# The first stage of a one-core decoder step: another order of loads, sessions and products

## The chip, the cores and the metric

The kernel runs on one core of one Trainium2 chip. The metric is the device time of one execution in microseconds; less is better. Three runs of the kernel before took 1009.87, 1010.07 and 1011.35 us, a median of 1010.07 us.

## The reference, cut to what matters

One layer of a hybrid decoder over 512 prompt tokens and 8 sample tokens (520 columns, D = 1024), all in float32:

```python
cs  = silu(c)                                   # 9 conditioning rows: 1 prompt, 8 samples
mod = cs @ w_mod + b_mod                        # (9, 6*1024): shift1, scale1, gate1, shift2, scale2, gate2
h   = rmsnorm(x, norm1_g) * (1 + scale1) + shift1
u   = h @ w_in                                  # 8 blocks of 1024 columns: q f i og x y ga gb
f   = lb + (1 - lb) * sigmoid(fa);  k = (1 - lb) * sigmoid(-fa);  q = silu(qa)
S_t = diag(f_t) S_{t-1} + k_t (x) v_t;  o_t = S_t^T q_t     # 8 heads of 128, v = ia
o_a = rmsnorm(o) * silu(oga);  o_b = RG-LRU(conv(xb)) * gelu(yb)
x   = x + gate1 * (sig(ga) * (o_a @ w_branch_a) + sig(gb) * (o_b @ w_branch_b)) @ w_out
x   = x + gate2 * (relu(h2 @ w_ff1)^2 @ w_ff2);  y = rmsnorm(x)   # h2 from x as h, with shift2, scale2
```

The part that concerns the change is everything up to `h` and the first column tiles of `u`.

## The kernel before, in words

Activations lie transposed: 8 feature columns (tiles k of 128 features on the partitions) by 520 tokens. A gemm makes one tile of 128 output features: 8 products, one per k, each of six matmuls. The operands are split into a high and a low part (`hi` is the rounded value, `lo` the rest), and a product is high by high, high by low and low by high, each over two halves of 260 tokens (`products`, L112). Weights come as tiles of 512 KB on the SP queue (`_load_w`), are cast to `whi` on ScalarE (L84) and subtracted to `wlo` on VectorE (L87), two tiles ahead of their gemm (`take_w`). The PSUM pool `pmm` has two buffers, so the third gemm needs the first one's result read.

The first stage (`begin`, L1579) makes `h` and the first two column tiles, which are f and q of head 0. SP loads c, x, then blocks of w_mod of 256 columns (1 MB each: scale1, part 1, and shift1, part 0, for two feature columns), with the two 512 KB tiles of w_in among them. ScalarE takes the squares of x, TensorE transposes x in pairs of feature columns (L462), VectorE takes the inverse root (L445 to L198); the root is transposed to all partitions (L470), copied (L474), and the columns are scaled by it (L477). Four conditioning sessions follow, one per pair of feature columns: 32 matmul records over two blocks of w_mod (L382), a copy to SBUF on ScalarE (L385), four transposes (L397) and reductions on VectorE (L402 to L409) give scale and shift. Then `affine_split` (L480) makes the pair's high columns on ScalarE (L490, tail L494), its full columns (L495) and low columns (L496) on VectorE. Between a session and its transposes stands the first of the last pair's four products, behind the transposes the other three. Only some orders are fixed, by dependencies without a wait (`behind`); the rest is set by the planner of the tile framework, which orders each engine's list by its own timeline.

Tiles of the stage lie in the pool `start`, which is closed at its end; the pool `hg` of the heads is opened over the same memory, and its first tiles wait for everything that read `start`. Then each head runs its gemms (f, q, output gate, v), sigmoids of f first (L157 by `head_f`), and leaves the rest of the recurrence to VectorE, ScalarE and small matmuls: v's copy (L549), its transposes and its broadcast over DRAM (`head_sample_v`), the decay levels (`level`, the last one ending in L618), the keys' transposes (L694). Parts that depend on them (`keys`, `states`, ...) are queued by `later(n, part)`, to be issued behind the n-th gemm from there. Two gemms of the RG-LRU branch stand between two heads.

Of the kernel before, what the change touches and what calls it, by code (L numbers as in the profile page):

```python
# [15 lines left out]
D = 1024  # L16
L = 512
# [13 lines left out]
NWM = 8  # L31
# [20 lines left out]
class Kernel:  # L52
    def __init__(self, ctx, tc, ins, outs):
        self.ctx, self.tc, self.nc = ctx, tc, tc.nc
        self.i, self.o = ins, outs
        self.group, self.sigmoids, self.mod_open = None, [], None
        self.ppt_free = True
        self.rg_pending = self.turn = self.last_hi = self.split_last = None
        self.late, self.ngemm = [], 0
# [18 lines left out]
    def _split_w(self, st, place, after=None, after_lo=None):  # L78
# [5 lines left out]
        ins = self.nc.scalar.copy(hi, st)  # L84
        if after:
            self.behind(ins, after)
        ins = self.nc.vector.tensor_tensor(lo, st, hi.bitcast(F32), OP.subtract)  # L87
        if after_lo:
            self.behind(ins, after_lo)
        return hi, lo  # L90

    def split_place(self):

        self.nsplit += 1
        self.places.append(self.nsplit % 4 if self.sw else 2 * (self.nsplit % 3))
        return self.places[-1]

    def take_w(self, key):
        n = self.wcur
        assert self.wspecs[n] == key, (n, self.wspecs[n], key)  # L100
        while self.wnext_split < min(n + AHEAD + 1, len(self.wspecs)):
# [7 lines left out]
        self.wcur += 1  # L109
        return self.wsplit.pop(n)  # L110
# [76 lines left out]
    def rsqrt_small(self, x, n, p=128, w=16):  # L187
# [4 lines left out]
        nc.vector.tensor_scalar(t.bitcast(I32), x.bitcast(I32), 1, None, OP.arith_shift_right)  # L192
        nc.vector.tensor_scalar(y.bitcast(I32), t.bitcast(I32), -1.0, float(0x5F3759DF), OP.mult, OP.add)
        nc.vector.tensor_scalar(h, x, -0.5, None, OP.mult)
        for _ in range(3):
            nc.vector.tensor_tensor(t, y, y, OP.mult)
            nc.vector.tensor_tensor(t, t, h, OP.mult)
            nc.vector.scalar_tensor_tensor(y, t, 1.5, y, OP.add, OP.mult)  # L198
# [39 lines left out]
    def transpose_in(self, out, rows, n):  # L238

        nc = self.nc  # L240
        ps = self.pps.tile([128, 512], F32, name="ps")
        nc.tensor.transpose(ps[:, :n], rows[:n, :], self.ident[:n, :n])
        nc.vector.tensor_copy(out, ps[:, :n])

# [9 lines left out]
    def bounds(self, r):  # L254

        nc = self.nc
        pl = self.hc.tile([128, 16], F32, name="pl")
        self.transpose_in(pl, r, 16)
        hl, lam = pl[:, 0:8], pl[:, 8:16]

        sb = self.hc
        t = sb.tile([128, 10, 8], F32, name="ptmp")
        mx, e, p, lb, na, ex, s, s2, acc, d = (t[:, j] for j in range(10))
        nc.vector.tensor_copy(mx, hl)
        nc.vector.tensor_tensor(e, hl, mx, OP.subtract)
        nc.vector.tensor_scalar(d, lam, -1.0, None, OP.mult)
        nc.vector.tensor_tensor(na, lam, d, OP.min)
        nc.scalar.activation(e, e, AF.Exp)
        self.exps = nc.scalar.activation(ex, na, AF.Exp)
        nc.vector.reciprocal(p, e)  # L270
        nc.vector.tensor_tensor(p, p, e, OP.mult)
        nc.vector.tensor_tensor(lb, p, p, OP.subtract)
        self.lbf, self.lb1, self.c8, self.c8n = (sb.tile([128, 8], F32, name=n) for n in ("lbf", "lb1", "c8", "c8n"))
        nc.vector.tensor_scalar(self.lbf, lb, 1e-30, None, OP.max)
        nc.vector.tensor_scalar(self.lb1, lb, -1.0, 1.0, OP.mult, OP.add)
        self.decay = ex, s, s2, acc, d

    def decays(self):
# [23 lines left out]
    def parameters_mod_in(self, r):  # L302
        pm = self.consts.tile([128, 64], F32, name="pm")
        self.transpose_in(pm, r, 64)
        self.bmod, self.n1g, self.n2g = pm[:, 0:48], pm[:, 48:56], pm[:, 56:64]
        for part in (1, 4):
            c = self.bmod[:, part * 8:part * 8 + 8]
            self.nc.vector.tensor_scalar(c, c, 1.0, None, OP.add)

# [16 lines left out]
    def parameters_in(self, ra, rb, rc):  # L326
        sb = self.hc
        pa = sb.tile([128, 57], F32, name="pa")
        pb = sb.tile([128, 64], F32, name="pb")
        pc = sb.tile([128, 192], F32, name="pc")  # L330
        self.transpose_in(pa, ra, 57)
        self.transpose_in(pb, rb, 64)
        for a in range(2):
            self.transpose_in(pc[:, a * 96:(a + 1) * 96], rc[:, a, :], 96)
# [3 lines left out]
        self.h0 = pb.rearrange("p (b k) -> p b k", b=NB)  # L338
        self.cbuf = pc.rearrange("p (b j k) -> p b j k", b=NB, j=3)


# [10 lines left out]
    def cond(self):  # L352
# [9 lines left out]
        nc.scalar.activation(ct, c, AF.Exp, scale=-1.0)  # L362
# [3 lines left out]
        self.modT = self.consts.tile([128, 48, NM], F32, name="modT")  # L366

# [6 lines left out]
    def mod(self, ws, ev, place):  # L374
# [3 lines left out]
        for j, w in enumerate(ws):  # L378
            n = w.shape[2]
            for k in range(KO):  # L380
                r = 32 * (k % 4)
                ins = nc.tensor.matmul(ps[r:r + 32, j * n:j * n + n], self.cT[:, k, :], w[:, k, :], start=k < 4, stop=k >= KO - 4)  # L382
                if self.ppt_free:
                    self.turn = self.behind(ins, self.turn) if self.turn else ins
        ins = nc.scalar.copy(ev, ps)  # L385
        if self.ppt_free and self.last_hi:
            self.behind(ins, self.last_hi)
        self.mod_open = ev, place

    def mod_close(self, after):  # L390
# [3 lines left out]
        pool, name = (self.ppt, "pt") if self.ppt_free else (self.pps, "ps")  # L394
        pt = pool.tile([128, 512], F32, name=name)
# [5 lines left out]
        for a in range(np):  # L401
            ins = nc.vector.tensor_reduce(out[:, a], got[:, a], mybir.AxisListType.X, OP.add)  # L402
            if self.ppt_free and self.split_last:
                self.behind(ins, self.split_last)
# [31 lines left out]
    def norm_x(self):  # L436
# [4 lines left out]
        nc.scalar.activation(junk[:NB], self.xsn, AF.Square, accum_out=ss[:NB, NC:NC + 1])  # L441
        for t in range(NC):
            last = nc.scalar.activation(junk, self.xn[:, t], AF.Square, accum_out=ss[:, t:t + 1])
        ss = ss[:, 0:8]
        nc.vector.tensor_scalar(ss, ss, 1.0 / D, EPS, OP.mult, OP.add)  # L445
        self.rs1 = self.rsqrt_small(ss, 8)
        return last

    def transposed(self):
# [4 lines left out]
        for k in range(KO):  # L454
            nc.tensor.transpose(ps[:, k * NB:(k + 1) * NB], self.xsn[:, k * 128:(k + 1) * 128], self.ident[:NB, :NB])
        for k in range(KO):
            nc.vector.tensor_copy(self.x[k][:, L:], ps[:, k * NB:(k + 1) * NB])
        for k in range(0, KO, 2):
            ps = self.pmm.tile([128, 2, 512], F32, name="mm")
            for j in range(2):  # L460
                for t in range(NC):
                    nc.tensor.transpose(ps[:, j, t * 128:(t + 1) * 128], self.xn[:, t, (k + j) * 128:(k + j + 1) * 128], self.ident)  # L462
                (nc.vector.tensor_copy if j else nc.scalar.copy)(self.x[k + j][:, :L], ps[:, j])

    def normed(self):

        nc, r = self.nc, self.rs1
        ps = self.ppb.tile([128, 512], F32, name="pb")
        for t in range(NC):
            nc.tensor.transpose(ps[:, t * 128:(t + 1) * 128], r[:, t:t + 1].to_broadcast([128, 128]), self.ident)  # L470
        p2 = self.pps.tile([128, 512], F32, name="ps")
        nc.tensor.transpose(p2[:, :NB], r[:NB, NC:NC + 1].to_broadcast([NB, 128]), self.ident[:NB, :NB])
        rsb = self.c128[:, :T]
        nc.scalar.copy(rsb[:, :L], ps)  # L474
        nc.vector.tensor_copy(rsb[:, L:], p2[:, :NB])
        for k in range(KO):
            nc.vector.tensor_tensor(self.u[:, k], self.x[k], rsb, OP.mult)  # L477

    def affine_split(self, k0):
# [1228 lines left out]
```

## Time and profile before

| what | value |
|---|---|
| median of three runs | 1010.07 us |
| the profiled execution's own time | 1010.27 us |
| its span, first to last instruction | 1008.5 us |
| mean granted TensorE clock | 0.994 |
| TensorE busy | 981.7 us, 97% |
| VectorE busy | 695.1 us, 69% |
| ScalarE busy | 515.8 us, 51% |

A page gives shares over the whole span. The stage of the change is only the first 50 us of it, so that stage is read from the timeline (start, duration, engine, line, what is written from what, count, and in brackets the idle time ahead and what ended it) and from the busy time in chosen stretches. Durations of a row that merges several instructions reach from the first start to the last end.

### The profile page before, as it was taken

To read this page: it belongs to the slowest core of one execution; us is meant where nothing else is said; L and a number is where in the kernel's file an instruction comes from. 1 tells how busy PE (TensorE), PEld (TensorE's weight loads), DVE (VectorE), ACT (ScalarE), POOL (GpSimd) and SP (SyncE) were. 2 spreads that over 40 slices of the span, in tenths; PEclk is the share of its full clock that TensorE was granted. 3 is DMA by queue.
4 is the path that set the end of the run, shared out by engine and by line. 5 is a ranking of instruction groups with operands and counts; after the bars stand their busy time and mean duration, and the time that the engine had idled before them with its cause. 6 is when DMAs were issued, how large, how long until landed. Compare 5 with 4: busy or idle time off the path is not lost.

```text
span 1008.5 us, 23267 instructions
## 1 busy us (share of the span) xinstructions
PE 981.7 (97%) x9585; PEld 955.3 (95%) x9585; DVE 695.1 (69%) x1547; ACT 515.8 (51%) x986; POOL 111.2 (11%) x194
## 2 busy tenths in 40 slices
PE   4999999999999999999999999999999999999996
PEld 3799999999999999999998999999999999999995
DVE  6768888698878868463233348767767776777685
ACT  5444764574565466351222224466556645646664
POOL 3000000000000000120000000022321331232051
PEclk9899999999999999999999999999999999999999
DMA  9794445354344434586566756322762483273142
GB/s 299 216 265 135 118 132 142 94 155 125 113 131 117 123 96 129 186 272 208 182 189 203 237 166 184 91 84 53 159 165 67 103 194 99 54 179 83 63 85 85
DMA packets 212572, 145.78 MB, mean 145 GB/s; under 512 B 6262, under 2 KB 196878, under 8 KB 212458
## 3 DMA queue, kind: packets, MB, share of 16 engines
q1 hardware_dynamic: 202562, 132.37, 44.4%
q0 software_dynamic: 9904, 11.92, 6.3%
q8 instruction: 75, 1.23, 0.5%
q14 instruction: 31, 0.25, 0.1%
HBM read 123.61 MB, written 13.39 MB: 136 GB/s over the span
## 4 chain that ended last, share of the span: by engine, by line
PE 91%; DVE 4%; DMA 3%; ACT 1%; issue 1%; SPq 0%; ACTq 0%; DVEq 0%; POOLq 0%
PE mm L118 65%; PE ps L1151 9%; PE pt L1151 4%; PE ps L382 2%; PE pb L1151 2%; PE pb L779 1%; PE ps L628 1%; DMA xn<-in_x_prompt_dram 1%; PE pt L704 1%; PE pt L717 1%; DMA wst<-in_w_in_dram 1%; DMA vb<-vd 1%; PE pt L628 1%; DMA st<-in_state_hgrn_dram 1%; PE pt L719 1%; DVE wlo L87 1%
## 5 line engine op out<-in xcount | busy, mean ns | idle before, releaser
L118 PE MATMUL mm<-h,whi 128*128 128x260 f32 (+1 forms) x3072 | 507.9, 285 | 1.9 <-ACT X L157 1.2
L118 PEld LDWEIGHTS mm<-h,whi 128*128 128x128 f32 x3072 | 425.9, 189 | 6.6 <-ACT whi L84 1.7
L118 PE MATMUL mm<-h,wlo 128*128 128x260 f32 (+1 forms) x1536 | 314.6, 284 | 0.0
L84 ACT CAST whi<-wst 128x1024 fp32r<-128x1024 f32 x166 | 173.7, 1048 | 209.2 <-PE mm L118 171.4
L87 DVE TENSOR_TENSOR wlo<-wst,whi 128x1024 fp32r<-128x1024 f32 x166 | 202.7, 1222 | 89.5 <-ACT whi L84 88.4
L118 PEld LDWEIGHTS mm<-h,wlo 128*128 128x128 f32 x1536 | 239.6, 189 | 0.1
L118 PE MATMUL mm<-a,whi 128*128 128x260 f32 x512 | 82.8, 283 | 0.0
L118 PEld LDWEIGHTS mm<-a,whi 128*128 128x128 f32 x512 | 70.3, 188 | 0.9 <-issue 0.8
L118 PE MATMUL mm<-a,wlo 128*128 128x260 f32 x256 | 51.7, 284 | 0.0
L1247 DVE TENSOR_TENSOR f<-f 128x260 f32<-128x260 f32 x64 | 27.3, 427 | 28.9 <-ACT f L1242 28.2
L880 POOL DMA_DIRECT2D t<-oaT_d x8 | 4.3, 547 | 375.6 <-ACT whi L84 369.0
L1236 ACT ACTIVATE ft<-ft,fsh 128x512 f32<-128x512 f32 (+2 forms) x36 | 24.1, 676 | 35.9 <-DVE ft L1233 35.9
L1239 POOL TENSOR_TENSOR ft<-ft,fsh 128x8 f32<-128x8 f32 x28 | 18.5, 659 | 216.0 <-DVE ft L1233 216.0
L118 PE MATMUL mm<-b,whi 128*128 128x260 f32 x256 | 41.6, 284 | 0.0
L118 PEld LDWEIGHTS mm<-a,wlo 128*128 128x128 f32 x256 | 39.4, 188 | 0.0
L118 PEld LDWEIGHTS mm<-b,whi 128*128 128x128 f32 x256 | 35.0, 188 | 2.5 <-issue 2.5
L614 DVE TENSOR_TENSOR Y<-Y,tb 128x512 f32<-128x512 f32 x40 | 27.5, 689 | 11.0 <-PE ps L628 5.5
L896 DVE TENSOR_TENSOR t<-mm,t 128x520 f32<-128x520 f32 x8 | 5.6, 700 | 37.0 <-PE mm L118 37.0
L1284 POOL DMA_DIRECT2D ma<-snap x28 | 26.6, 950 | 39.1 <-issue 22.1
L1263 POOL DMA_DIRECT2D ma<-snap x28 | 26.6, 950 | 39.0 <-DMA ma<-snap 23.3
L1242 ACT ACTIVATE f<-ft 128x520 f32<-128x520 f32 (+1 forms) x36 | 20.8, 587 | 15.0 <-POOL ft L1240 12.9
L573 ACT ACTIVATE st<-st,fkq 128x128 f32<-128x128 f32 x64 | 19.6, 389 | 13.8 <-DVE fkq L553 12.8
(477 smaller groups left out, 1820.9 us busy)
## 6 DMA issues: line engine op xcount, KB each, us to landing
wst<-in_w_in_dram SPq DMA_DIRECT2D x64, 512.0 KB
wm<-in_w_mod_dram SPq DMA_DIRECT2D x8, 2048.0 KB
wst<-in_w_ff_dram SPq DMA_DIRECT2D x64, 256.0 KB
wst<-in_w_ff_dram SPq DMA_DIRECT2D x32, 512.0 KB
wm<-in_w_mod_dram SPq DMA_DIRECT2D x8, 1024.0 KB
st<-in_state_hgrn_dram SPq DMA_DIRECT2D x8, 512.0 KB
vb<-vd SPq DMA_DIRECT2D x8, 512.0 KB
out_dram<-st SPq DMA_DIRECT2D x8, 512.0 KB
```

What stands on the lines that cost most here:

```text
L84: ins = self.nc.scalar.copy(hi, st)
L87: ins = self.nc.vector.tensor_tensor(lo, st, hi.bitcast(F32), OP.subtract)
L118: self.last_product = self.nc.tensor.matmul(ps[:, s, :c.stop - c.start], x, y[:, c], start=first and n == 0, stop=last and n == 2)
L382: ins = nc.tensor.matmul(ps[r:r + 32, j * n:j * n + n], self.cT[:, k, :], w[:, k, :], start=k < 4, stop=k >= KO - 4)
L614: made = nc.vector.tensor_tensor(view(Y, b, 0, 2 * b, n, b), view(X, b, 0, 2 * b, n, b), fac, OP.mult)
L628: ins = nc.tensor.matmul(*args, start=True, stop=True)
L1151: ins = self.nc.tensor.matmul(ps, x[:, w], y[:, f], start=j in (1, 7, 2) and k == 0 and n == 0, stop=k == 3 and n == 2, skip_group_check=True)
L1236: nc.scalar.activation(t[:, :p], t[:, :p], AF.Relu, bias=sh[:, 0:1])
L1242: nc.scalar.activation(f, self.two(self.ft)[:, a:a + n], AF.Square)
L1247: self.nc.vector.tensor_tensor(f[:, n], f[:, a], f[:, b], op)
L1263: nc.gpsimd.dma_start(x[1][:, b], v[:, :n], accum_op=OP.add)
L1284: nc.gpsimd.dma_start(x[t][:, a], s[p], accum_op=OP.add)
```

## The change

The order of the first stage is written out: every instruction of it on TensorE, VectorE and ScalarE is put behind the one before it on its engine, by a function `order`. The first two column tiles are f of heads 0 and 1 instead of f and q of head 0, loaded by one transfer of 1 MB; head 0 then has the gemms q, output gate and v, head 1 the same. The loads come in the order scale and shift of columns 0 and 1, the two gates, scale and shift of columns 2 and 3, scale of columns 4 to 7 as one block of 2 MB, shift of 4 and 5, shift of 6 and 7, and sessions follow them: one block with several columns or two blocks. Six feature columns of x are transposed as the rows arrive, and the first pool of the heads waits tile by tile. The diff's core ("..." is what is left out: the same calls wrapped in `order`, and the four parameter transposes brought together in one PSUM tile and one copy):

```diff
     def split_place(self):
-        self.places.append(self.nsplit % 4 if self.sw else 2 * (self.nsplit % 3))
+        self.places.append(self.nsplit % 4 if self.sw else 2 * ((self.nsplit - 1) % 3))
...
+    def bounds(self, pl, order):
...
+        def exps():
+            order("a", nc.scalar.activation(e, e, AF.Exp))
+            order("a", nc.scalar.activation(ex, na, AF.Exp))
+        def ends():
...
+    def transposed(self, between, order):
...
+        mm = [self.pmm.tile([128, 2, 512], F32, name="mm") for _ in range(2)]
+        rows = [mm[0][:, 0], mm[0][:, 1], mm[1][:, 0], mm[1][:, 1],
+                self.ppb.tile([128, 512], F32, name="pb"), self.ppt.tile([128, 512], F32, name="pt")]
+        for t in range(NC):
+            for k, p in enumerate(rows):
+                order("p", nc.tensor.transpose(p[:, t * 128:(t + 1) * 128], self.xn[:, t, k * 128:(k + 1) * 128], self.ident))
+            if t == 2:
+                between()
...
+    def normed(self, ss, rows, order):
+        self.copied("v", 4, rows[4], order)
+        order("v", nc.vector.tensor_scalar(ss, ss, 1.0 / D, EPS, OP.mult, OP.add))
+        r = self.rsqrt_small(ss, 8, order=order)
+        for k in (0, 1):
+            self.copied("a", k, rows[k], order)
+        for k in (2, 3):
+            self.copied("v", k, rows[k], order)
...
+    def affine_split(self, k0, order, between=lambda j: None):
...
+        hi(0)
+        full(0)
+        order("a", nc.scalar.copy(self.h_hi[:, ks, L:T], f[:, :, L:]))
+        hi(1)
+        between(0)
+        full(1)
+        lo(0)
+        lo(1)
+        between(1)
...
     def head(self, h):
-        f, X = self.head_f(h, first[0] if first else self.gemm(kf, self.h)[:, :, :HALF])
-        q = self.head_q(X[:, 2], first[1] if first else self.gemm(kq, self.h)[:, :, :HALF])
+        f, X = self.first_f[h] if h < 2 else self.head_f(h, self.gemm(kf, self.h)[:, :, :HALF])
+        q = self.head_q(X[:, 2], self.gemm(kq, self.h)[:, :, :HALF])
...
     def head_sample(self, h, st, vb, fkq, after):
-            nc.scalar.activation(st[:, b], st[:, b], AF.Copy, scale=fkq[:, 0, b:b + 1])
+            self.behind(nc.scalar.activation(st[:, b], st[:, b], AF.Copy, scale=fkq[:, 0, b:b + 1]), self.vcopy)
...
-        self.later(3, keys)
+        self.later(3 if h else 2, keys)
...
     def begin(self):
+        load(1, 0, 2)
+        load(0, 0, 2)
+        raw = self.start.tile([128, KO, 256], F32, name="wf")
+        nc.sync.dma_start(raw, self.i["w_in"][0][:, D:D + 256].rearrange("(k p) n -> p k n", p=128))
+        load(1, 2, 2)
+        load(0, 2, 2)
+        load(1, 4, 4)
+        load(0, 4, 2)
+        load(0, 6, 2)
...
+        scaled(0, 1)
+        bounds_end()
+        scaled(2, 3)
+        a = session((1, 0), (0, 0))
+        closed(*a)
+        high(0)
...
+        self.affine_split(0, order, weights)
+        products((0, 0), (0, 1), (1, 0), (1, 1))
+        scaled(4, 5)
+        a = session((1, 2), (0, 2))
+        closed(*a)
+        self.affine_split(2, order)
+        self.parameters_in(*par, order)
+        scaled(6, 7)
+        products((0, 2), (1, 2))
+        a = session((1, 4))
+        products((0, 3), (1, 3))
+        closed(*a)
+        a = session((0, 4))
+        closed(*a)
+        self.affine_split(4, order)
+        a = session((0, 6))
+        products((0, 4))
+        closed(*a)
+        self.affine_split(6, order)
+        products((1, 4), (0, 5), (1, 5), (0, 6), (0, 7), (1, 6), (1, 7))
+        self.last_hi, self.split_last = ends["a"], ends["v"]
         self.decays()
         self.close_pool()
-        self.hg = self.open_pool("hg", 2)
+        self.whe = self.early.enter_context(self.tc.tile_pool(name="whe", bufs=1))
+        self.hg = self.open_pool("hg", 2, reuse_waits="tile")
+        self.first_f = [self.head_f(h, acc[h][:, :, :HALF]) for h in range(2)]
```

`session` multiplies its blocks with the conditioning rows on TensorE and copies the sums on ScalarE; `closed` transposes the copy and reduces each block on VectorE, block by block (reduction, bias, and for the scale a factor). `products((j, k), ...)` are the six matmuls of gate j and column k. `high(j)` and `low(j)` split gate j's weights; `weights` calls `low(0)` in the middle of the first `affine_split` and `high(1)` and `low(1)` at its end. `ends` of `bounds` are five small operations. The small pool `whe` for one in three weight tiles, opened with the others before, is now opened behind the stage.

## Rows read from the trace of the kernel before

**Rows 1.** Page: busy us (share) and instructions; granted TensorE clock in 40 slices.
```profile
PE 981.7 (97%) x9585; PEld 955.3 (95%) x9585; DVE 695.1 (69%) x1547; ACT 515.8 (51%) x986; POOL 111.2 (11%) x194
...
PEclk9899999999999999999999999999999999999999
```

**Rows 2.** Busy time by stretch, TensorE: length, PE busy (instructions), clock, DMA, GB/s.
```profile
0.00:51.50 51.50, 35.80 (x299) 0.93 0.83 254
51.50:110.00 58.50, 58.05 (x662) 1.00 0.63 181
110.00:1000.00 890.00, 887.84 (x8626) 1.00 0.49 135
```

**Rows 3.** Timeline, root and scaled columns: start, us, engine, line, operation.
```profile
12.32 0.17 DVE L445 TENSOR_SCALAR ss<-ss 128x8 f32<-128x8 f32 x1 [3.60 <-ACT ht L443]
...
15.89 0.17 DVE L198 SCALAR_TENSOR_TENSOR rs_y<-rs_t,rs_y 128x8 f32<-128x8 f32 x1
...
17.45 0.59 ACT L474 COPY c<-pb 128x512 f32<-128x512 f32 x1
...
17.96 1.29 DVE L463 COPY ma<-mm 128x512 f32<-128x512 f32 x2 [1.90 <-PE mm L462]
...
21.41 3.70 DVE L477 TENSOR_TENSOR xn<-ma,c 128x520 f32<-128x520 f32 x6
```

**Rows 4.** Timeline, second weight tile, first session's copy, second session.
```profile
24.31 1.04 ACT L1598 CAST whi<-wst 128x1024 fp32r<-128x1024 f32 x1 [1.71 <-DMA wst<-in_w_in_dram]
...
25.27 0.58 ACT L385 COPY modev<-ps 128x512 f32<-128x512 f32 x1
...
26.24 1.22 DVE L1599 TENSOR_TENSOR wlo<-wst,whi 128x1024 fp32r<-128x1024 f32 x1
...
27.49 3.52 PE L382 MATMUL ps<-wm,cT 128*32 128x256 f32 x32 [0.47 <-DVE wlo L1599]
```

**Rows 5.** Busy time by stretch, TensorE, around the gap; columns as in rows 2.
```profile
20.00:21.46 1.46, 1.46 (x28) 1.00 1.12 329
21.46:25.89 4.43, 0.01 (x2) 0.78 1.13 330
...
27.49:31.01 3.52, 3.52 (x33) 0.54 1.09 349
```

**Rows 6.** Timeline, one round: transposes, closing, high, full and low columns, next session.
```profile
31.76 0.66 PE L397 MATMUL pt<-ident,modev 128*128 128x128 f32 x4
...
32.46 0.37 DVE L402 TENSOR_REDUCE modT<-pt 128x18 f32<-128x72 f32 x2 [1.35 <-PE pt L397]
...
33.30 0.82 ACT L490 ACTIVATE h<-xn,modT 128x512 fp32r<-128x512 f32 x1 [1.60 <-DVE modT L409]
...
33.40 1.00 DVE L495 TENSOR_SCALAR ht<-xn,modT 128x512 f32<-128x512 f32 x2
...
34.50 1.93 PE L382 MATMUL ps<-wm,cT 128*32 128x256 f32 x32
...
34.75 1.42 DVE L496 TENSOR_TENSOR h<-ht,h 128x520 fp32r<-128x520 f32 x2 [0.27 <-ACT h L494]
```

**Rows 7.** Chain of waits, last products of the stage: start, us, what.
```profile
47.36 2.92 PE mm L118 x22
```

**Rows 8.** Timeline, first sigmoid of f and next gemm.
```profile
50.36 0.60 ACT L157 ACTIVATE e<-mm 128x520 f32<-128x520 f32 x1 [1.45 <-PE mm L118]
...
51.51 0.74 PE L118 MATMUL mm<-h,whi 128*128 128x260 f32 x4 [1.24 <-ACT X L157]
```

**Rows 9.** Timeline, head 0: v's copy, K's last part, keys' transposes.
```profile
63.34 0.59 ACT L549 COPY e<-mm 128x520 f32<-128x520 f32 x1 [2.68 <-PE mm L118]
...
82.29 0.41 DVE L618 COPY X<-Y 128x512 f32<-128x512 f32 x1
...
84.49 0.49 PE L694 MATMUL pt<-ident,X 128*128 128x128 f32 x3
```

**Rows 10.** Tile xn, its readers: duration in ns min/median/max, starts.
```profile
L462 PEld LDWEIGHTS mm<-ident,xn x32: 139/224/231, 6.6 to 17.9; 128*128 128x128 f32 x32
```

More of the change, by code (lines that the diff above doesn't have):

```diff
@@ L381, in mod @@
                 r = 32 * (k % 4)
[L382 to L387, printed above, removed]
+                nc.tensor.matmul(ps[r:r + 32, j * n:j * n + n], self.cT[:, k, :], w[:, k, :], start=k < 4, stop=k >= KO - 4)
+        nc.scalar.copy(ev, ps)
         self.mod_open = ev, place
@@ L454, in transposed @@
         for k in range(KO):
-            nc.tensor.transpose(ps[:, k * NB:(k + 1) * NB], self.xsn[:, k * 128:(k + 1) * 128], self.ident[:NB, :NB])
+            order("p", nc.tensor.transpose(ps[:, k * NB:(k + 1) * NB], self.xsn[:, k * 128:(k + 1) * 128], self.ident[:NB, :NB]))
         for k in range(KO):
[L457 to L463, printed above, removed]
@@ L528, in head_q, with head @@
         return q
-    def head(self, h, first=None):
+    def head(self, h):
         nc = self.nc
@@ L1611, in begin, with load @@
-        for k in (4, 6):
-            load_mod(1, k)
-            load_mod(0, k)
-        squares = self.norm_x()
-        self.transposed()
-        self.bounds(pl)
-        self.parameters_mod_in(pm)
-        self.normed()
-        ready = nc.scalar.activation(self.act0, self.act0, AF.Sigmoid)
-        self.behind(self.behind(ready, squares), self.exps)
-        first = [first_w(st) for st in staged]
-        par = self.parameters()
+        loaded = {}
+        def load(part, k, n):
+            loaded[part, k] = w = self.start.tile([128, KO, n * 128], F32, name=f"wm{part}{k}")
+            c = part * D + k * 128
+            nc.sync.dma_start(w, self.i["w_mod"][0][:, c:c + n * 128].rearrange("(k p) n -> p k n", p=128))
@@ new lines, in session @@
+        def session(*parts):
+            ws = [loaded.pop(x) for x in parts]
+            n = ws[0].shape[2]
+            ps = self.pps.tile([128, 512], F32, name="ps")[:, :n * len(ws)]
+            for j, w in enumerate(ws):
+                for k in range(KO):
+                    r = 32 * (k % 4)
+                    order("p", nc.tensor.matmul(ps[r:r + 32, j * n:j * n + n], self.cT[:, k, :], w[:, k, :],
+                                                start=k < 4, stop=k >= KO - 4))
+            ev = self.sm.tile([128, 512], F32, name="modev", bufs=1)[:, :n * len(ws)]
+            order("a", nc.scalar.copy(ev, ps))
+            return ev, parts, n // 128
@@ new lines, in begin @@
+        load(1, 0, 2)
[7 more added lines that the diff above has]
+        load(0, 6, 2)
+        first = [[self.start.tile([128, KO, 128], F32R, name=f"w{n}{j}") for n in ("hi", "lo")] for j in range(2)]
+        part = lambda j: raw[:, :, j * 128:j * 128 + 128]
@@ new lines, in begin, with parameters @@
+        high = lambda j: order("a", nc.scalar.copy(first[j][0], part(j)))
+        low = lambda j: order("v", nc.vector.tensor_tensor(first[j][1], part(j), first[j][0].bitcast(F32), OP.subtract))
+        order("a", self.cond())
+        ss = self.norm_x(order)
+        bounds = []
+        def parameters():
+            bounds.append(self.parameters_first(pl, pm, order))
+        rows = self.transposed(parameters, order)
+        exps, bounds_end = self.bounds(bounds[0], order)
+        exps()
@@ L1639, in begin, with weights @@
-        products(sorted(todo))
-        self.parameters_in(*par)
+                self.products(acc[j], (wh[:, k], wl[:, k]), self.h[k], k == 0, k == KO - 1, after=ends["p"])
+                ends["p"] = self.last_product
+        def weights(j):
+            if j == 0:
+                low(0)
+            else:
+                high(1)
+                low(1)
+        self.affine_split(0, order, weights)
+        products((0, 0), (0, 1), (1, 0), (1, 1))
+        scaled(4, 5)
+        a = session((1, 2), (0, 2))
@@ L1650, in begin @@
         nc.gpsimd.memset(self.at, 0.0)
-    def head_start(self, h):
-        self.head(h, [ps[:, :, :HALF] for ps in self.first])
     def end_recurrences(self):
```

233 lines of the change are left out of this document (110 added, 123 removed).

## The prediction

> **What bounds the kernel now.** I read the page first: TensorE is busy for 97% of the span, at a granted clock of nine tenths or more in all of the 40 slices but the second [rows 1]. The busy time by stretch then shows where the rest lies: 35.80 of 51.50 us in the first stage, 58.05 of 58.50 in the next stretch, 887.84 of 890 after that [rows 2]. Behind 51.5 us, then, TensorE has some 2.6 us of idle time up to the end of its work, and the change neither adds nor removes a matmul. What the kernel can win or lose is the moment at which the gapless stream of gemms starts, plus any stall that it gets in the first two heads. Before, that moment is 51.51 us [rows 8]: two of the 64 w_in column tiles are then done. Afterwards two are done again (f of heads 0 and 1 instead of f and q of head 0), so the same work is left and the difference of the two moments is the difference of the spans.
>
> The timeline shows what the first stage does before. The second weight tile's cast on ScalarE waits for its load until 24.31; the copy of the first conditioning session stands behind it and runs at 25.27, though the session was over by 21.46 [rows 4, 5]. In that gap TensorE idles for 4.43 us and its granted clock falls to 0.50; the second session takes 3.52 us where a later one takes 1.93 [rows 4 to 6]. From 27.49 on TensorE is nearly gapless up to the last product at 50.28 [rows 7]. Then comes a hole: the first sigmoid of f runs only at 50.36 and the next gemm at 51.51 [rows 8].
>
> **The change, step by step.** All TensorE work of the stage stays: the five new sessions hold as many columns as the four old ones (1.93 twice, then 1.93 and two halves of 0.95), and transposes and products are equal in number. So I follow the new order on each engine with the durations before.
>
> *Up to the scaled columns.* Before, 12.32 starts the root and 16.06 ends it, with two copies of 0.65 each between: 2.45 net [rows 3]. Now one copy stands ahead: 12.32 + 0.65 + 2.45 = 15.4. From there to the copy of the broadcast root it was 17.45 - 16.06 = 1.4, and the copy 0.59: 17.4. Four scaled columns at 3.70 / 6 = 0.62 and five small operations of 0.17 make 3.35: VectorE is free at 20.75. Session one (1.93, from about 17), its copy (0.58) and its transposes (0.66) are over at some 20.3 and hide behind that, with half a microsecond to spare [rows 3, 4, 6].
>
> *The joint load.* Before, the second tile was there at 24.31 with 4.19 MB behind x; now both gates are there with 3.15 MB. At about 330 GB/s [rows 5] the missing 1.05 MB is 3.2 us: 21.1. The high part takes 1.03 and ends at 22.1. The later loads have the same bytes ahead as before: the second pair by 27.4, the wide scale block by 33.5, the last block by 39.6 at some 347 GB/s [rows 5]. All come before TensorE asks for them below, so DMA isn't the bound.
>
> *First products.* Closing takes 33.30 - 32.46 = 0.84 before [rows 6]; one dependent step more makes it 0.95, an estimate. VectorE from 21.7: full column 0.5, low weights 1.2, full column 0.5, two low columns of 0.65 to 0.7 each, low weights of gate two 1.2 [rows 4, 6]: low column one at 24.6, two at 25.3, the last low weights at 26.5. TensorE, idle from about 20.3 but for two matmuls, starts its run of 22 at 24.6. I take the clock as half then (1.2 of 2.4 GHz), because the 4.43 us gap before halved it. It rose again at 30.73 (the mean of 0.54 over 27.49 to 31.01 gives that), 3.24 after work resumed [rows 5]. So it rises at 27.85: 13 matmuls at 0.244 by then, nine at 0.122 after it, end at 28.9. (0.122 is the spacing in the 22 of 2.92 [rows 7]; 0.244 is an estimate, twice that.) Session two follows at once: 28.9 + 1.9 = 30.8. That is where it ended before (31.01), but with 24 products' matmuls done that came later before.
>
> *From the end E of session two.* Before, products lay between a session and its transposes; now the transposes follow directly, so TensorE waits for the copy: 0.75. Transposes end at E + 1.3, closing at 2.25, high column one at 3.1, full columns at 3.45, low ones at 4.15 and 4.8. The parameter transposes fill 0.6 of this. Products (0,2) finish at 4.65, (1,2) 5.4, the wide session 7.3, products of column three 8.75, transposes 9.25, half session 10.2, wait for its copy to 10.95, two transposes 11.2, last half session 12.15. The half close takes 0.45, so low column four comes at 13.65: product (0,4) 14.2, two transposes 14.45, three products 16.65; low column six at 16.9: (0,6) 17.45, (0,7) 18.2, and the other two 19.65. Within these are 4.85 us of waits (0.75 + 2.0 + 0.75 + 1.3 + 0.05); this is what the earlier start of the products is paid with.
>
> *The hole at the end.* Gate 0 is ready at E + 18.2, and with a tile-wise pool its two sigmoids (0.60 each [rows 8]) run while (1,6) and (1,7) go on: bank free at 19.4. Before, they stood behind the last product, and the next gemm 1.24 behind it. I leave 0.15 for a weight cast in front of them. So the stream starts at E + 19.8 = 50.6, 0.9 earlier than 51.51. Bounds: the clock at full throughout (27.5 by the low weights, E = 29.4) gives 49.2; at half for all 22 matmuls and the whole session (3.52) E = 33.5 and 53.3. I take 50.6, because it uses the recovery that the row shows.
>
> *Edits at nothing.* The parameter copies, merged into one, and the earlier parameter loads: VectorE has room at E + 4.8, and those loads go on the POOL queue, where they ran early anyway. If that cover fails, one copy of some 0.4 delays the scaled columns six and seven, which nothing needs until E + 15. The early-weights pool opened later, with the shifted places, is first used for the third weight tile, 11.8 us ahead of need. The ScalarE edge behind the v copy orders only state work.
>
> *A rule against it.* Load-weights of the early x transposes took 224 ns at the median and 139 at the least, with a granted clock shown as 1.00 [rows 1, 5, 10]. The Trainium skill, "TensorE: Matmul & The Clock Gate", Part 1: The HAM clock gate, says that half rate is the default and that only sustained work lifts it; by that, and these durations agree, early transposes spread out by arrival of x could leave session one at half rate. This is rival 2.
>
> **The sum.** The profiled execution took 1010.27, span 1008.5, 1.77 around it. 1010.27 - 0.9 = 1009.4. The profiled run is 0.2 above the median of 1010.07, so this is 0.7 below the median. 0.2% is 2.0 us: about what a measurement of this kernel can tell from no change.
>
> **Rivals.**
> 1. *The clock stays up* (or comes back within a microsecond). For: the new gap has two matmuls inside and starts after a denser stretch. Against: 4.43 us was enough before. Session two ends at 29.4 and the stream starts at 49.2: -2.3, 1008.0.
> 2. *Session one at half rate.* It runs 17 to 20.5, is copied by 21.1 and transposed at half rate (1.1) by 22.2; closing starts 1.5 later than at 20.75. All else shifts: 52.1, +0.6, 1010.9. For: rows 10. Against: before, the transposes were spread out too, and still 28 of session one's 32 records fit into 1.46 us [rows 5], full rate.
> 3. *The pool frees nothing.* The sigmoid's tile lies where the last products' weights lay, and still waits for (1,7): +1.24, 1010.6. The diff asks for tile-wise waits, so only the placement could do this.
> 4. *Slower: keys of head 0 come late.* v of head 0 is now the third gemm of the stream, not the second; its keys still come after the fifth. Before, v was copied at 63.34, K ready at 82.70 and used from 84.49 on [rows 9]. Now v comes at 50.6 + 17.7 = 68.3, 5.0 later; if all behind it moves with it K is ready at 87.7, while TensorE asks at 50.6 + 33.0 = 83.6: a wait of 4.1, 1013.5. It turns the kernel slower by over 0.2% from a wait of 2.7 on. Against: 19.4 us from v's copy to K is far more than the work between them, so part of it was queueing and need not move (none of it moving is the other end, no wait); and the planner may put other matmuls ahead of keys that it sees come late.
>
> **How the numbers follow.** Forecast 0.42 (its own range 1008.2 to 1011.2: waits 4.85 a quarter off, the rise of the clock some 1.5 either way); rival 1 0.26; rival 2 0.10; rival 3 0.10; rival 4 0.12. Under 1008.05: 0.20 of rival 1 and 0.11 of the forecast. Over 1012.1: 0.09 of rival 4, 0.03 each of rivals 2 and 3 (with some of 4 on top), 0.04 of the forecast at its latest clock. That makes 0.31, 0.50 and 0.19. The range runs from rival 1 with a quarter less waiting, 1006.8, put at 1006.6, to 1012.6, between the half-clock bound (53.3, 1012.1) and rival 4.
>
> **What would show it.** First product's run at 24.6 and session two's end near 30.8; granted clock 0.5 for some stretch between 22 and 29; the first sigmoid of f before the last product; q of head 0 gapless at 50.6. A stream that starts before 49 says that the waits of 4.85 are overstated; one past 52.5, that an in-order engine waits for something that I hid. A busy time of TensorE under 57.5 in the 58.5 us behind the start would show rival 4.

## The result: slower by 0.4%, outside the predicted range

The median after is 1014.27 us over five runs (1013.77 to 1014.85), against 1010.23 before in the same comparison (1009.87 to 1011.35). The ratio is 1.0039, 95% interval 1.0028 to 1.0049. The forecast was 1009.4 with a range up to 1012.6, so the prediction was wrong in sign. The profiled execution after took 1013.78 us with a span of 1012.0, 3.5 more than before.

The page of the kernel after, its lines on busy time and on granted clock:

```profile
PE 984.6 (97%) x9569; PEld 956.4 (95%) x9569; DVE 691.4 (68%) x1544; ACT 514.1 (51%) x988; POOL 111.2 (11%) x194
...
PEclk8899999999999999999999999999999999999998
```

Beside [rows 1], TensorE is 2.9 us longer busy for the same products, and the first slice's clock is lower. The stretches of [rows 2], now after the change (length, busy time of each engine, then granted clock, DMA share and GB/s):

```profile
0.00:51.50 51.50, 36.63 (x268) 26.29 (x269) 33.20 (x125) 24.03 (x44) 8.68 (x23) 0.87 0.78 252
51.50:110.00 58.50, 56.88 (x654) 56.24 (x653) 45.54 (x125) 25.55 (x49) 0.00 (x0) 1.00 0.63 182
110.00:1000.00 890.00, 888.71 (x8635) 871.96 (x8634) 606.12 (x1274) 460.15 (x883) 99.66 (x170) 1.00 0.48 135
```

The mean clock of the first stage is 0.87 where it was 0.93. The next stretch is no longer full: 56.88 against 58.05. Behind 110 us nothing is lost. So there are two places to look at, the stage and the first head. The timeline of the kernel after (columns as in [rows 3]; L121 are products, L1619 sessions, L160 sigmoids):

```profile
17.98 1.07 PE L1619 MATMUL ps<-wm,cT 128*32 128x256 f32 x16 [0.94 <-DMA wm<-in_w_mod_dram]
...
20.98 1.04 ACT L1650 CAST whi<-wf 128x1024 fp32r<-128x1024 f32 x1 [1.27 <-DMA wf<-in_w_in_dram]
...
24.46 0.80 PE L121 MATMUL mm<-h,whi 128*128 128x260 f32 x2 [1.07 <-DVE h L496]
...
29.53 2.08 PE L1619 MATMUL ps<-wm,cT 128*32 128x256 f32 x32
...
32.38 0.66 PE L1628 MATMUL pt<-ident,modev 128*128 128x128 f32 x4 [0.77 <-ACT modev L1622]
...
34.99 0.51 PE L121 MATMUL mm<-h,whi 128*128 128x260 f32 x2 [1.37 <-ACT h L493]
...
35.96 0.50 PE L121 MATMUL mm<-h,whi 128*128 128x260 f32 x2 [0.47 <-DVE h L496]
...
37.82 3.04 PE L1619 MATMUL ps<-wm,cT 128*32 128x512 f32 x16
...
52.19 0.59 ACT L160 ACTIVATE e<-mm 128x520 f32<-128x520 f32 x1
...
53.35 0.72 PE L121 MATMUL mm<-h,whi 128*128 128x260 f32 x4
...
72.63 0.72 PE L121 MATMUL mm<-h,whi 128*128 128x260 f32 x4 [1.61 <-DVE e L550]
```

Session two ends at 29.53 + 2.08 = 31.61. The wide session takes 3.04 us. The stream starts at 53.35 (q of head 0, right behind the last product), which is 1.84 later than the 51.51 of [rows 8]. The hole that stood there is gone, since the sigmoid of f runs at 52.19 beside the last products. Then the fourth gemm of the stream, the first of the RG-LRU branch, waits 1.61 us at 72.63 for the product of head 0's output gate (L550), which frees its PSUM buffer. 1.84 + 1.61 = 3.45 is about the whole difference of the spans, 3.5 (a wait of 0.44 at 85.42 before is gone, and some 0.4 lies elsewhere).

Why the wide session is slow stands in the granted clock of short stretches (columns as above):

```profile
13.00:16.00 3.00, 3.00 (x17) 2.39 (x20) 2.50 (x10) 1.45 (x4) 0.00 (x0) 0.50 1.09 319
...
29.50:30.00 0.50, 0.50 (x9) 0.28 (x12) 0.00 (x0) 0.00 (x0) 0.00 (x0) 0.62 1.03 381
...
36.00:36.50 0.50, 0.50 (x4) 0.50 (x5) 0.50 (x2) 0.00 (x0) 0.00 (x0) 1.00 1.11 336
36.50:37.00 0.50, 0.50 (x5) 0.50 (x4) 0.50 (x3) 0.00 (x0) 0.00 (x0) 0.70 1.16 316
...
40.00:40.50 0.50, 0.50 (x8) 0.00 (x0) 0.00 (x0) 0.00 (x0) 0.00 (x0) 0.88 0.31 76
...
31.61:36.00 4.39, 1.78 (x11) 1.16 (x11) 2.79 (x11) 2.21 (x4) 0.00 (x0) 1.00 1.09 348
```

The clock rose from 1.2 to 2.4 GHz in the half microsecond from 29.5, and fell again at about 36.7, to come back only behind 40. Ahead of the second fall TensorE had been busy for 1.78 of 4.39 us, in pieces between waits of 0.77, 1.37 and 0.47: no gap as long as the 4.43 of [rows 5], but many. The clock had also been at 0.50 from 13 to 16 us. Nothing shows that this cost time: the second half of session one is held by its load until 17.98 and then runs at full rate. So it isn't counted below, where "the second fall" is the one at 36.7.

Why the gate's product is late stands in the lists of the other engines, in the kernel after, back from the stall (SPq is the SP engine's DMA queue):

```profile
28.47 24.53 SPq L73 DMA_DIRECT2D wst<-in_w_in_dram  x3
...
65.91 0.30 ACT L771 CAST bdhlru_wa<-bdst 128x128 fp32r<-128x128 f32 x1 [3.19 <-DMA bdst<-in_lru_wa_dram]
...
68.23 0.65 ACT L623 COPY Y<-X 128x512 f32<-128x512 f32 x1 [1.82 <-DVE Y L621]
...
69.73 0.59 ACT L160 ACTIVATE e<-mm 128x520 f32<-128x520 f32 x1
...
71.73 0.75 DVE L550 SCALAR_TENSOR_TENSOR e<-mm,pa,e 128x520 f32<-128x520 f32 x1
```

The gate's gemm was over by 65, but its sigmoid runs at 69.73. ScalarE goes through its list in order, and ahead of that sigmoid stands the cast of a 64 KB block-diagonal weight (`bdst`) that isn't there until 65.91. The three issues merged in the first row end at 53.00: the third weight load waits for a staging buffer (there are two, and VectorE reads that of the first weight until 52.60, for the low part). All other loads stand behind it on SP.

### The profile page after: what moved, and what is told of

It reads as the page before. It is cut to its first block, busy times and chain, and to the rows that moved or that the text cites. A ratio compares the mean times of both kernels' runs of the same rounds, so it can differ in the third digit from the quotient of the medians.

```text
span 1012.0 us, 23217 instructions
## 1 busy us (share of the span) xinstructions
PE 984.6 (97%) x9569; PEld 956.4 (95%) x9569; DVE 691.4 (68%) x1544; ACT 514.1 (51%) x988; POOL 111.2 (11%) x194
## 4 chain that ended last, share of the span: by engine, by line
PE 91%; DVE 4%; DMA 2%; ACT 1%; issue 1%; SPq 0%; ACTq 0%
PE mm L121 65%; PE ps L1158 9%; PE pt L1158 4%; PE pb L1158 2%; PE ps L635 2%; PE ps L384 1%; DMA wm<-in_w_mod_dram 1%; PE pb L786 1%; PE pt L724 1%; PE ps L1619 1%; PE pt L635 1%; PE pt L711 1%; DMA bdst<-in_lru_wa_dram 1%; PE pt L726 1%; DVE wlo L85 1%
## 5 line engine op out<-in xcount | busy, mean ns | idle before, releaser
L121 PE MATMUL mm<-h,whi 128*128 128x260 f32 (+1 forms) x3072 | 510.4, 286 | 7.8 <-ACT h L493 4.1
L121 PEld LDWEIGHTS mm<-h,whi 128*128 128x128 f32 x3072 | 427.6, 189 | 13.8 <-ACT h L493 5.0
L121 PE MATMUL mm<-h,wlo 128*128 128x260 f32 (+1 forms) x1536 | 314.9, 285 | 0.0
L121 PEld LDWEIGHTS mm<-h,wlo 128*128 128x128 f32 x1536 | 240.7, 190 | 0.0
L121 PE MATMUL mm<-a,whi 128*128 128x260 f32 x512 | 82.8, 283 | 0.0
L121 PEld LDWEIGHTS mm<-a,whi 128*128 128x128 f32 x512 | 70.3, 188 | 0.9 <-issue 0.8
L121 PE MATMUL mm<-a,wlo 128*128 128x260 f32 x256 | 51.7, 284 | 0.0
L121 PE MATMUL mm<-b,whi 128*128 128x260 f32 x256 | 41.6, 284 | 0.0
L121 PEld LDWEIGHTS mm<-a,wlo 128*128 128x128 f32 x256 | 39.4, 188 | 0.0
L121 PEld LDWEIGHTS mm<-b,whi 128*128 128x128 f32 x256 | 35.0, 188 | 2.5 <-issue 2.5
L121 PE MATMUL mm<-b,wlo 128*128 128x260 f32 x128 | 25.8, 283 | 0.0
```

The costliest lines, as they stand in the source:

```text
L121: self.last_product = self.nc.tensor.matmul(ps[:, s, :c.stop - c.start], x, y[:, c], start=first and n == 0, stop=last and n == 2)
```

## Experiments

The theory: two costs that I had left out. **A1**: the clock falls a second time in the waits behind session two. **A2**: head 0's chain on ScalarE and VectorE stands, in order, behind small loads that are late on SP. Two rivals: the start of the stream sets the time alone (then only the stage matters), or the cost lies in the tile-wise pool. Each kernel ran 5 to 11 times; traces are of one execution each.

### Keep TensorE at work behind session two

```diff
+        def fill(n):
+            t = self.ppb.tile([128, 512], F32, name="pb")
+            for _ in range(n):
+                order("p", nc.tensor.transpose(t[:, :128], self.x[0][:, :128], self.ident))
         a = session((1, 2), (0, 2))
+        fill(6)
         closed(*a)
         self.affine_split(2, order)
         self.parameters_in(*par, order)
+        fill(12)
```

The 18 transposes are extra, and nobody reads them. Expected:

> The changed kernel with 18 more transposes of a finished column into an idle PSUM bank, nobody reads them: 6 behind the second session, 12 behind the parameter transposes, about as long as TensorE's waits there (0.77 and 1.37 us). Theory A: these waits make the granted clock fall at 36.7, so the wide session takes 3.04 instead of 1.93 and the products around it run at half rate; with the fill the clock stays at 1.00 from 30 to 42, the wide session takes 1.9, q of head 0 starts at about 51.6 instead of 53.35, and the time falls by 1.5 to 2 us. Rival B: the stage's end is set by the chain through VectorE and ScalarE, not by the clock; the added work then changes nothing or costs up to 1 us.

Measured: 1012.14 (ratio to before 1.0016, 1.0007 to 1.0025). Its timeline and the clock of three of its stretches:

```profile
28.29 1.93 PE L1619 MATMUL ps<-wm,cT 128*32 128x256 f32 x32
...
50.39 0.71 PE L121 MATMUL mm<-h,whi 128*128 128x260 f32 x4
...
60.48 0.59 ACT L160 ACTIVATE X<-mm 128x520 f32<-128x520 f32 x1
...
63.35 0.72 PE L121 MATMUL mm<-h,whi 128*128 128x260 f32 x4 [1.20 <-issue]
```

```profile
25.50:27.00 1.50, 1.50 (x8) 1.50 (x8) 1.45 (x3) 0.00 (x0) 0.00 (x0) 0.50 1.05 386
27.00:27.50 0.50, 0.50 (x5) 0.50 (x5) 0.00 (x0) 0.00 (x0) 0.00 (x0) 0.79 1.05 389
...
36.00:38.00 2.00, 2.00 (x18) 0.56 (x18) 0.74 (x2) 0.00 (x0) 0.00 (x0) 1.00 1.16 311
```

Useless work made the kernel faster, by 2.1 us at the median: the clock stays at 1.00 through the wide session, which takes 1.92, and the stream starts at 50.39 instead of 53.35. The lists of ScalarE, VectorE and SP are those of the change. Nor is the second fall an accident of one execution. In the four traces without this fill (the change and three kernels below) the clock is at 0.50 in the wide session, which takes 3.04, 3.21, 2.45 and 2.97; in the four with it, 1.92 each. So A1 is shown.

In this execution the first rise also came earlier, at 27.2 and not at 29.9, which the edit doesn't reach (in the other three traces without a filled first gap it came at 29.1 to 29.8). So 31.61 - 30.22 = 1.4 of the 2.96 belong to the first rise and some 1.6 to the second fall. The profiled execution is the fastest of eleven, 2.9 us under that of the change, so its start can't be set against the median. In it the stall at 72.63 has shrunk to 0.25, at 69.61, and a new one of 1.20 stands at 63.35: q's sigmoid, at 60.48, stands behind a `bdst` cast at 59.32.

### The same in both gaps

The 18 transposes, and 34 more (`fill(34)`) ahead of the first products.

> As the first, with 34 more such transposes (3.9 us) between the first session's transposes and the first products, where TensorE idles from 20.4 to 24.5 but for two matmuls. Theory A: the clock doesn't fall at 23 either, the first 22 matmuls end near 27.3, the second session near 29.3 instead of 31.6, q of head 0 starts near 49.5, 4 us less than the changed kernel. Rival B: the first products stay bound by the low columns and low weights, and the start of q moves by less than 1 us against the run with one fill.

Measured: 1010.19 (0.9995, 0.9986 to 1.0004), no different from before. The clock is full in the first gap too, and the start is 50.12 (the first row is session one):

```profile
16.75 2.94 PE L1619 MATMUL ps<-wm,cT 128*32 128x256 f32 x32
```

```profile
21.00:24.50 3.50, 3.50 (x34) 3.50 (x33) 3.26 (x11) 2.87 (x5) 0.00 (x0) 1.00 1.09 347
```

The profiled execution, with 1011.97, was the longest of eleven and had stalls of 1.50 at 63.39 and 0.82 at 70.21. With both gaps filled the stage is 1.4 us shorter than before, and the kernel isn't: an early stream runs into head 0's lists. Session one was slow in this execution (2.94, where 1.93 is full rate), so VectorE began to close it at 21.10. The two other kernels with this stage, below, began at 20.00 and 19.77, and their streams started at 48.99 and 48.76.

### The gate ahead of the small casts

Here `og0` is the sigmoid of head 0's output gate and its product; "..." stands for the lines that keep them.

```diff
...
+            cast = nc.scalar.copy(hi, st)
             last = nc.vector.tensor_tensor(lo, st, hi.bitcast(F32), OP.subtract)
             if n < 2:
                 self.behind(last, self.split_last)
+                self.behind(cast, self.og0[0])
+                self.behind(last, self.og0[1])
```

> The changed kernel with one more order: the casts and low parts of the block-diagonal weights of the first two RG-LRU blocks stand behind the sigmoid and product of head 0's output gate on ScalarE and VectorE. Theory A: the stall of 1.61 us at 72.6 comes from ScalarE, which waits until 65.9 for a 64 KB load with that sigmoid behind it; with the order turned the sigmoid runs at about 65, the stall goes, and the time falls by 1.6 us; start of q stays at 53.35. Rival B: VectorE is late there for its own work (level operations, low weights); the stall stays above 1 us.

Measured: 1012.85 (1.0025, 1.0016 to 1.0034), by the medians 1.4 less than the change. Timeline of this kernel:

```profile
53.08 0.75 PE L121 MATMUL mm<-h,whi 128*128 128x260 f32 x4
...
66.71 0.60 ACT L160 ACTIVATE e<-mm 128x520 f32<-128x520 f32 x1
67.20 0.29 ACT L773 CAST bdhlru_wa<-bdst 128x128 fp32r<-128x128 f32 x1
...
92.50 0.39 PE L790 MATMUL pb<-xcs,bdhlru_wa 128*128 128x260 f32 x1 [0.77 <-ACT xcs L186]
```

The sigmoid moves from 69.73 to 66.71 and the stall at 72.63 is gone, with the start where it was. That shows A2. With this edit the planner also issues the second block's small loads later on SP. Half of the stall comes back at 92.50, where the RG-LRU block waits for its own operand; the profiled executions differ by 1.1.

### The loads on another queue

```diff
-            nc.sync.dma_start(st, self.i[name][0, n])
+            (nc.gpsimd if n < 2 else nc.sync).dma_start(st, self.i[name][0, n])
```

> The changed kernel with the loads of the block-diagonal weights of the first two RG-LRU blocks (64 KB each) issued on the POOL queue in place of SP's, where they stand behind weight loads that wait for buffers until 53 us. Theory A (the 1.61 us stall at 72.63 hangs on the late landing of these loads): the casts on ScalarE no longer wait 3.19 us at 65.9, the gate's sigmoid comes before 69, the stall is under 0.4; q of head 0 still starts at 53.1 to 53.5; time 0.8 to 1.6 us under the changed kernel's, 1012.7 to 1013.5. Rival B (ScalarE and VectorE have too much work there, whatever the loads do): the stall stays at 1.2 to 1.8 and the time at 1013.8 to 1014.6. Rival C (stall goes, another wait takes its place between 74 and 93): stall under 0.4, new wait of 0.8 or more there, time within 0.6 of the changed kernel's.

Measured: 1015.30 (1.0050, 1.0038 to 1.0063), by the medians 1.0 above the change, though the intervals overlap; outside all that was expected. The timeline:

```profile
41.58 0.55 POOL L768 DMA_DIRECT2D bdst<-in_lru_wx_dram  x1
65.21 0.54 POOL L768 DMA_DIRECT2D bdst<-in_lru_wa_dram  x1 [23.09 <-DVE bdllru_wa L772]
...
70.47 0.30 ACT L771 CAST bdhlru_wa<-bdst 128x128 fp32r<-128x128 f32 x1 [2.59 <-DMA bdst<-in_lru_wa_dram]
...
71.62 0.60 ACT L160 ACTIVATE e<-mm 128x520 f32<-128x520 f32 x1
...
74.39 0.73 PE L121 MATMUL mm<-h,whi 128*128 128x260 f32 x4 [2.77 <-DVE e L550]
```

I had overlooked that `bdst` has two buffers. The first block's loads are now early, but their casts were placed behind q's weight cast, so the second block's load gets its buffer only at 65.21 and lands at 70.4 instead of 65.9. As a test of A2 this is the opposite dose, though not a clean one, as the first block's casts moved too: the load comes 4.5 later, the sigmoid 1.9 later, and the stall grows from 1.61 to 2.77. The same edit in the kernel with both gaps filled:

> The same queue for these loads in the kernel with 52 useless transposes in both gaps (median 1010.2, start of q about 50.1, stalls 1.50 at 63.4 and 0.8 at 70.2). Theory A: both stalls under 0.5, since q's sigmoid and the gate's stand behind casts of these weights; time 1008.0 to 1009.2. Rival C: stalls gone, waits for the conv samples of block 0 between 85 and 93 of 0.9 to 2 us in their place; time 1009.2 to 1010.3. Rival B: stalls as they were, 1010.0 to 1010.6.

Measured: 1013.79 (1.0038, 1.0025 to 1.0052), none of the three expected. By the medians the fills gain 1.5 here, against 4.1 on the change itself; the intervals with and without them overlap. Its timeline and two stretches:

```profile
48.76 0.74 PE L121 MATMUL mm<-h,whi 128*128 128x260 f32 x4
...
62.15 0.71 PE L121 MATMUL mm<-h,whi 128*128 128x260 f32 x4 [1.60 <-issue]
...
70.69 0.96 PE L121 MATMUL mm<-h,whi 128*128 128x260 f32 x4 [2.53 <-DVE e L550]
```

```profile
71.00:73.00 2.00, 2.00 (x12) 2.00 (x11) 2.00 (x5) 0.00 (x0) 0.00 (x0) 0.50 0.95 251
73.00:75.00 2.00, 2.00 (x13) 2.00 (x13) 0.28 (x1) 0.00 (x0) 0.00 (x0) 0.65 0.40 111
```

The start is 4.6 earlier than with the change alone, and stalls of 1.60 and 2.53 take most of it. Behind the second one the clock falls in the middle of the stream, which costs another 2.0 x 0.5 + 2.0 x 0.35 = 1.7.

### The gate order with both gaps filled

> The changed kernel with both fills and with the gate order of the third experiment. Theory A (two independent costs: the clock in the first stage, and ScalarE standing behind 64 KB loads in head 0): the start of q near 50.1 as with both fills, and the waits of the second and third gemm behind it (1.5 and 0.8 us) go; the time falls by 1.5 to 2 us against both fills, to about 1008.5, below the kernel before. Rival B (the first heads are held by something later, such as the loads themselves): another wait of about the same length appears, and the time stays near 1010.2.

Measured: 1010.17 (0.9997, 0.9988 to 1.0006). Start 48.99; neither stall at 62 nor at 70; new waits of 1.19 at 74.83 (VectorE in order behind the second block's low part, whose load lands at 73.7) and 0.94 at 90.28 (the RG-LRU operand). So rival B held: another wait of about the same length.

### The tile-wise pool alone, both ways

In the kernel before, only the pool of the heads made tile-wise (`reuse_waits="tile"`), with every engine's list the same; and in the changed kernel, that pool made ordinary again.

> The kernel before with one part of the change alone: the heads' pool waits tile by tile. The lists of all engines are the same, only waits differ. Theory A: the hole from 50.28 to 51.51 was the pool's wait, so the first sigmoid of f runs at about 49, before the last product, and the time falls by 1.2 us. Rival B: another wait of the same sigmoids keeps the hole, and nothing changes.

> The changed kernel with the heads' pool waiting for everything again; the lists of all engines are the same. Theory A (head 0's gate sigmoid is held by loads, not by TensorE): the hole comes back, so q of head 0 starts some 1.2 us later, at about 54.5, but the stall of 1.61 shrinks by about as much, and the time stays within 0.5 us of the changed kernel's. Rival B (the start of the stream is the bound and the stall is its own): the time grows by 1.2 us, to 1015.5.

The kernel before with the tile-wise pool took 1011.89 (1.0013, 1.0005 to 1.0022), slower than without, although its stream starts 2.1 earlier (0.7 of it from an earlier stage in this execution: the last products begin at 46.68 and not at 47.36). Its timeline:

```profile
48.25 0.61 ACT L157 ACTIVATE e<-mm 128x520 f32<-128x520 f32 x1
...
49.44 0.71 PE L118 MATMUL mm<-h,whi 128*128 128x260 f32 x4
...
62.93 0.73 PE L118 MATMUL mm<-h,whi 128*128 128x260 f32 x4 [1.73 <-DVE e L543]
```

The changed kernel without it took 1013.27 (1.0031, 1.0021 to 1.0042), by the medians 1.0 less than with it, though the hole is back. The two intervals overlap, so this is at most no loss:

```profile
54.11 0.75 PE L121 MATMUL mm<-h,whi 128*128 128x260 f32 x4 [1.24 <-ACT X L160]
...
72.14 0.72 PE L121 MATMUL mm<-h,whi 128*128 128x260 f32 x4 [0.49 <-DVE e L550]
```

In both pairs the stall grows as the hole goes: 1.24 plus nothing against 1.73 in the one, 1.24 and 0.49 against 1.61 in the other. This speaks against the start of the stream as the only bound, and for a chain in head 0 with a pace of its own. The pool itself does what it should: with it the sigmoid of f runs at 48.25, beside the last products. Start and stall alone don't make the first kernel slower (2.1 less, 1.7 more); 1.0 of its longer span is one more wait, at 437.66 us, for a sigmoid on ScalarE.

### What the best order gives

The kernel before with the tile-wise pool, the gate order of above, and the state's scaling behind v's copy; and the same with 36 unread transposes in the gap of [rows 5].

> The kernel before with the tile-wise pool, and with two orders on ScalarE and VectorE: the state's scaling behind the copy of v (a part of the change), the casts of the first two blocks' block-diagonal weights behind head 0's output gate. Theory A: the hole of 1.24 is gone as with the pool alone, and the stall of 1.73 before the third gemm goes too, because the gate's sigmoid no longer stands behind loads; 1.2 to 2 us less than before, 1008.5 to 1009. Rival B: the stall stays or moves, as with the pool alone, and the time is 1010.4 or more.

> As the seventh, with 36 transposes that nobody reads in the gap of 4.4 us between the first session and its transposes. Theory A: the granted clock stays at 1.00, the second session takes 1.9 instead of 3.5, the stream starts 1.5 us earlier than in the seventh, and the time falls by 1 to 1.5 us more, to about 1007.5. Rival B: loads hold head 0, the earlier start turns into a wait, and the time is that of the seventh.

Measured: 1010.57 (1.0001, 0.9992 to 1.0010) and 1009.28 (0.9993, 0.9984 to 1.0002): neither can be told from before. They start at 49.70 and 49.38, and lose 1.95 at 85.65 in the one, 0.76 at 61.91 and 1.63 at 85.47 in the other, to the gate and the RG-LRU operand. In the second the clock is full and session two takes 1.93 for 3.27, so it ends 1.3 us earlier (29.24 against 30.57). But the sessions behind it then wait for their loads, and only 0.3 of this reaches the start:

```profile
33.22 1.93 PE L382 MATMUL ps<-wm,cT 128*32 128x256 f32 x32 [0.36 <-DMA wm<-in_w_mod_dram]
...
39.24 1.93 PE L382 MATMUL ps<-wm,cT 128*32 128x256 f32 x32 [0.49 <-DMA wm<-in_w_mod_dram]
...
85.47 0.39 PE L783 MATMUL pb<-xcs,bdhlru_wa 128*128 128x260 f32 x1 [1.63 <-ACT xcs L183]
```

So in the order of before the loads stand close behind the clock: of the 1.3 us given back, the start kept 0.3.

### The sum over all kernels

Start of the stream, TensorE's larger waits from there to 110 us, and what is left of the span, from the profiled executions. (Three of these lie away from their kernel's median: that filled behind session two 1.3 us under it, that filled in both gaps 1.8 over, that with pool and orders 0.85 under.)

| kernel | start | waits | span | span - start - waits |
|---|---|---|---|---|
| before | 51.51 | 0.44 | 1008.5 | 956.6 |
| after | 53.35 | 1.61 | 1012.0 | 957.0 |
| filled behind session two | 50.39 | 1.45 | 1009.1 | 957.3 |
| filled in both gaps | 50.12 | 2.32 | 1010.2 | 957.8 |
| gate first | 53.08 | 0.77 | 1010.8 | 957.0 |
| filled, gate first | 48.99 | 2.13 | 1008.4 | 957.3 |
| loads on another queue | 53.16 | 3.47 | 1013.5 | 956.9 |
| the same, filled | 48.76 | 4.13 and 1.7 of clock | 1011.3 | 956.7 |
| after, ordinary pool | 54.11 | 0.49 | 1011.5 | 956.9 |
| before, tile-wise pool | 49.44 | 2.11 | 1009.7 | 958.2 |
| before, pool and orders | 49.70 | 1.95 | 1007.9 | 956.3 |
| the same, filled | 49.38 | 2.39 | 1007.5 | 955.7 |

The last column stays within 1.3 us of 957, while the starts differ by 5.4. So the frame of the prediction, start plus stalls, holds; what fills it didn't. That last microsecond isn't explained, but for the 1.0 at 437.66 in the row of the tile-wise pool.

## Why the prediction was wrong

**The step that failed** is "From the end E of session two": "Within these are 4.85 us of waits", priced as waits only. The waits themselves were about as priced: those that the timeline names sum to 4.0 (0.77, 1.37, 0.47, 0.55, 0.39, 0.46), and without the 1.6 that follows the way from E to the start is 20.1, against 19.8. But cut up by them, TensorE lost the clock once more: the wide session took 3.04 for 1.93, and the products ahead of it 0.92 and 0.64 for 0.64 and 0.40, together 1.6. From E to the start it was 21.7 instead of 19.8. The recovery behind the first gap, a mis-sized term, came at 29.9 and not at 27.85, so E was 31.61 instead of 30.8. Together 0.8 + 1.9 = 2.7, from 50.6 to 53.35. With the stall of the next paragraph, 1.61, this turns the -0.9 of the forecast into about the +3.5 of the spans. I had carried over one rise of the clock from [rows 5] and then held it for granted, with rows of the same kind of gap in front of me. The bound at half clock (53.3) was for a late rise, and met the number by luck: the late rise is only 0.8 of the 2.7.

**The second term left out** is the stall of 1.61 in head 0. "What the kernel can win or lose is the moment at which the gapless stream of gemms starts, plus any stall" was the right frame, and the stall was then set to nothing in the sum. I had looked at TensorE's waits behind 51.5 us, and not at how closely it missed one. In the timeline of the kernel before these two rows stand together:

```profile
62.22 0.75 DVE L543 SCALAR_TENSOR_TENSOR e<-mm,pa,e 128x520 f32<-128x520 f32 x1
...
63.14 0.69 PE L118 MATMUL mm<-h,whi 128*128 128x260 f32 x4
```

The gate's product ends at 62.97, and the third gemm, which takes the PSUM buffer that it frees, starts at 63.14: 0.17 us to spare. Whatever starts the stream earlier must move the gate's chain as well, or wait there. The change moved the chain later, as SP was free for other loads at 53.0 and not at 49.7.

**Rival 4** had the side and the head right and the place wrong. No wait of TensorE in that stretch is for the keys; it is the output gate's PSUM buffer, which comes free late, at the fourth gemm. v's later place did no harm that shows.

**The other rivals.** Rival 1 fell, the clock went down in the first gap as well. Rival 2 did not decide this execution: the clock was at half until some 16.2, into the first half of session one, but the second half took 1.07, full rate, and VectorE began to close it at 20.45, where I had it free at 20.75. In the execution with both gaps filled the rival did hold: session one took 2.94, although the view shows a clock of 1.00 there, so a 1.00 this early can't be taken as measured. Rival 3 fell with the sigmoid at 52.19.

**What held.** The cast of the joint load came at 20.98 (21.1 forecast), the first product's run at 24.46 (24.6), and the hole went. The sign of a stream past 52.5, "that an in-order engine waits for something that I hid", pointed the wrong way for the stage, which the clock delayed, and the right way for the stall behind it.

**What is shown and what is argued.** Shown by experiment: the second fall of the clock and its price, and the order of ScalarE's and VectorE's lists behind the small loads as cause of the 1.61. Argued from rows: that these loads are late because SP waits for a staging buffer until 53.00. A third buffer was not tried. Open: which of loads and lists would have to give for a start ahead of 50 to pay.

## What to carry to other kernels

Where an order trades one long gap for several short ones, price them at the granted clock and not only in waiting time, and look at the row behind each earlier gap of that kind. And before an earlier start is counted as a gain, check that the engines and queues behind it run ahead of it: here, in six kernels whose stream started 1.1 to 2.5 us earlier than before, 1.0 to 2.0 us more of waits stood 10 to 40 us behind the start. A small transfer at the head of an in-order list can hold up a large chain.

## What was not expected of the hardware

TensorE's granted clock fell to half after a stretch with 1.78 us of work in 4.39 and no single wait over 1.37 us. Unread transposes in the gaps kept it up and made the kernel 2.1 and 4.1 us faster than the change alone. A stall of 2.53 us in the middle of the stream was followed by a clock of 0.50 for over 2 us, while one of 2.77 in the sister kernel was not: the next matmuls there ran at the full 0.73 for four.
